# One copy, a reordered entry and an earlier split: three edits at the transitions of a fused recurrence, attention and projection kernel

## The chip, the cores and the metric

The kernel runs on one core of a Trainium2 chip. The metric is the device time of one execution in microseconds (us), as the median of several runs. Names of engines: PE is TensorE (PEld its weight loads), DVE is VectorE, ACT is ScalarE, POOL is GpSimd, SP is SyncE, which here issues nearly all DMA transfers. Each engine works through its own instructions in order; semaphores make one wait for another.

## The reference

One layer on x of 2048 tokens by 1024 (a grid of 32 rows by 64 columns), float32:

```python
mod = silu(c) @ ada_w + ada_b                    # shift, scale, gate
h = layernorm(x) * (1 + scale) + shift
proj = h @ w_in                                  # 1024 -> 9216 columns
q_h, i_h, zf_fw, zf_bw, g_h, q_n, k_n, v_n, g_n = split(proj)

# HGRN2, 8 heads of 128, forward and backward in time, in chunks of 32 tokens
f = lb + (1 - lb) * sigmoid(zf);  k = 1 - f
state = decay * state + k_end^T v                # per chunk
o = q_inter @ state + tril(q k^T) v              # decays folded into q and k
y_hg = rmsnorm(o_fw + o_bw) * silu(g_h)

# neighbourhood attention, 16 heads of 64, windows of 8 x 16 inside the grid
s = q k^T / 8 + bias (masked);  p = softmax(s)
y_na = (p @ v) * silu(g_n)

y = concat(y_hg, y_na) @ w_out                   # 2048 -> 1024
out = layernorm(alpha * x + gate * y) * ln_g + ln_b
```

## The kernel before

Float32 products are made from a high and a low half of each operand: three matmuls (high x high, high x low, low x high) of 128 x 128 by 512 or 256 columns. ScalarE makes the high half by a copy (`wh`, `yh`, `wo`, L268, L1460, L1428), VectorE the low half by a subtraction (`wl`, `yl`, L269, L1461, L1429).

The program has five stages: layernorm, modulation and the first half of attention (to about 530 us); 16 HGRN units, 8 heads times two halves of the sequence (530 to 1740); the second half of attention, 8 units of two heads (1740 to 2296); and the output projection, whose first four row tiles run inside the last attention unit.

**Who sets the order.** PE's instructions run in the order in which the program writes them (`manual_schedule`). A function `weave` advances two generators in turn: a mixer (one HGRN or attention unit) and a stream of dense matmuls (projections of the next unit), so that the dense ones fill PE while the mixer waits for other engines. The instructions of ACT, DVE and SP are ordered by a scheduler with priorities; `tc.high_priority(offset=PRI)` puts one ahead, and `pinned` (which is `keep_in_program_order`) keeps it in the order of the program with the other pinned ones of its engine.

**The first HGRN unit.** `hgrn` works in two groups g of four chunks of 128 tokens. `turned` (L472, L474) transposes the decayed keys into `ke`. `updates` (L480) multiplies ke and v for four chunks into one PSUM tile "pu", of which there is one buffer. `forward_states` (L485 to L494) then makes four states on DVE: the first one by a copy (L493), the others by decay times the state before plus the chunk's part of "pu" (L491). A second `updates` for the other direction needs the same buffer, and so comes after the fourth state step. In between stand `diagonal_factors` (kx and qx, L504 to L510) and after it `diagonal` (L519); then come `level` (L547), `masked` (pm, L560) and `outputs` (L571, L573).

**The second half of attention.** A unit `Prep` has q, k and gate prepared from projection results (`q`: L950 and L951, `k`: L966 and L967, `gate`: L984 to L986), and loads its value tiles (`v`: L977). `alone` (L758) makes Z, a copy of one head's queries. `vproj` projects the values (L291): eight steps of 24 matmuls at a pair of heads' columns, each four steps ending with two evacuations `vt` (L297). `vstream` gives these steps one by one; before attention starts, five of them run, in the middle of which two evacuations come. Then `natten_woven` walks through 16 places (R, j) per unit: `scores` (L1029 to L1036 on PE, bias and maximum on DVE L1045, exponential on ACT L1050, normalising on DVE L1055), two places later `turned` (transposes of the probabilities, L1078, copied to pt on DVE L1082 and ACT L1084) and `sums` (L1100). Tables of places call further work in between (`extra`):

```python
extra = {..., 7: [(wo_split, 0, 0, 1)], 8: [(wo_split, 0, 2, 3), (wo_load, 0, 6, 7)],
         9: [(wo_split, 0, 4, 5)], 10: [(wo_load, 1, 0, 1, 4, 5), (y_early, 0)], 11: [(y_early, 1)]}
```

**The start of the output projection.** `y_early` (L1434) loads the gated results y of one row tile as two pieces from DRAM, `y_split` (L1460, L1461) halves them, `wo_load` and `wo_split` (L1428, L1429) do the same for w_out. The matmuls of y (L1468 to L1470) are the dense stream of attention's last unit, u = 7. Both of the first tiles are split at the start of that unit.

Of the kernel before, what the change touches and what calls it, by code (L numbers as in the profile page):

```python
# [13 lines left out]
AF = mybir.ActivationFunctionType  # L14
# [16 lines left out]
PRI = 1500  # L31
# [7 lines left out]
def body(ctx: ExitStack, tc: tile.TileContext, t):  # L39
    nc = tc.nc  # L40
    dve, act, pool, pe = nc.vector, nc.scalar, nc.gpsimd, nc.tensor
    dma = nc.sync.dma_start
    x, out = t["x"], t["out"]
# [236 lines left out]
    def vproj(src, dst, half, feed=None, fine=False):  # L280
        his, los = feed.take(4) if feed else load_split(lambda i: src[:, i * 512:(i + 1) * 512], 4)
        for t2 in range(2):
            pzs = [ps("pj"), ps("pj")]
            for k in range(KT):
                wh, wl = (w[k // 2][:, (k % 2) * 256:(k % 2 + 1) * 256] for w in (his, los))
                for tp in range(2):
                    for i in range(2):
                        g, o = divmod(((t2 * 2 + tp) * 2 + i) * P, GRP)
                        hh, hl = (hts[g, k, s][:, o:o + P] for s in range(2))
                        for n, (a, b) in enumerate(((hh, wh), (hh, wl), (hl, wh))):  # L290
                            pe.matmul(pzs[tp][:, i * 256:(i + 1) * 256], a, b, start=(k == 0 and n == 0 and i == 0), stop=(k == KT - 1 and n == 2), skip_group_check=True)  # L291
                if k % 2:
                    if k == KT - 1:
                        for tp, pz in enumerate(pzs):
                            v = tl("vo")
                            with tc.high_priority(offset=PRI):
                                act.activation(v, pz, AF.Copy)  # L297
                                r0 = half * HALF + (t2 * 2 + tp) * 256
                                dma(dst[r0:r0 + 256].rearrange("(i p) c -> p i c", p=P), v.rearrange("p (i c) -> p i c", c=256))
                    if feed and t2:  # L300
                        feed.free(1)
                if fine or k % 2:
                    yield None
# [117 lines left out]
    def hgrn(u, half, st, tail):  # L421
# [55 lines left out]
        def updates(ke, v):  # L477
            pu = ps("pu")
            for b in range(4):
                pe.matmul(pu[:, b * P:(b + 1) * P], ke[:, b * P:(b + 1) * P], v[:, b * P:(b + 1) * P], start=True, stop=True)  # L480
            return pu
# [94 lines left out]
        for g in range(2):  # L576
            v = turned(vts[g], "v")
            next(tail, None)
            cs, ks = {}, {}
            cs[0], ks[0] = rates(0, g)  # L580
            yield 5
            next(tail, None)
            cs[1], ks[1] = rates(1, g)
            de0 = ends(0, g, cs[0], ks[0])
            yield 5
            next(tail, None)
            ke0 = turned(de0, "ke")
            de1 = ends(1, g, cs[1], ks[1])
            kx, qx = diagonal_factors(g, cs, ks)
            yield 3  # L590
            next(tail, None)
            forward_states(g, updates(ke0, v))
            ke1 = turned(de1, "ke")
            yield 3
            next(tail, None)
            pu = updates(ke1, v)
            if g == 0:
                ub = tl("ub")
                act.activation(ub, pu, AF.Copy)
                ubs[g] = ub  # L600
            else:
                ubs[g] = pu
            pb = diagonal(kx, qx)
            lf = [(w, *level_factors(w, g, cs, ks)) for w in (32, 64)]
            yield 6
            next(tail, None)
            pa = ps("pa")
            for w, xk, xq in lf:
                level(w, pa, xk, xq)
            pm = masked(pa, pb)  # L610
            yield 5
            outputs(g, v, pm)
# [139 lines left out]
    def alone(st, R):  # L752

        z = keysets[0]["Z"]
        with tc.high_priority(offset=PRI):
            for hh in range(2):
                hs_ = slice(hh * 64, hh * 64 + 64)
                act.activation(z[hs_, hh * 512:(hh + 1) * 512], st.Q[R][hh][hs_], AF.Copy)  # L758

    NCOL = (("q", 5120), ("k", 6144), ("g", 8192))  # L760
    NCOL0 = (("k", 6144), ("q", 5120), ("g", 8192))
# [140 lines left out]
    NLEN = 2 * len(NCOL) * KT * KUS  # L902
    VLEN = 8 * 2.9
# [22 lines left out]
    class Prep:  # L926


        def __init__(self, p, half, raws):
            self.p, self.half, self.raws = p, half, raws  # L930
            self.Q, self.V, self.sg, self.bias, self.bk = {}, {}, {}, {}, {}

        def fetch(self, name):
# [10 lines left out]
        def q(self, R):  # L944
            raw = self.src("q", R)
            rv = raw.rearrange("p (r j c) -> p j r c", j=4, c=16)[:, :, ::-1, :]
            a, b = tl("Q", F32R), tl("Q", F32R)
            av, bv = (z.rearrange("p (j r c) -> p j r c", j=4, c=16) for z in (a, b))
            keep = pinned if raw is self.bk.get("q") else lambda x: x
            keep(act.activation(av[0:64], rv[0:64], AF.Copy))  # L950
            keep(act.activation(bv[64:128], rv[64:128], AF.Copy))  # L951
            dve.tensor_tensor(av[64:128], rv[0:64], av[0:64], op=ALU.subtract)
            dve.tensor_tensor(bv[0:64], rv[64:128], bv[64:128], op=ALU.subtract)
            self.Q[R] = (a, b)

        def k(self, i):
            a, b, src, off = KPIECE[self.half][i]
            n = (b - a) * GW
            raw = (self.bk[src] if src in self.bk else self.raws["k"][src])[:, off:off + n]
            o = slice(a * GW, b * GW)  # L960
            top, bot = slice(0, 64), slice(64, 128)
            keys = keysets[self.p % len(keysets)]
            keep = pinned if src in self.bk else lambda x: x
            for z, x, y in (("KA", top, bot), ("KB", bot, top)):
                z = keys[z]
                keep(act.activation(z[x, o], raw[x], AF.Copy))  # L966
                dma(z[y, o].bitcast(F32), z[x, o].bitcast(F32))  # L967
                dve.tensor_tensor(keys["KL"][x, o], raw[x], z[x, o], op=ALU.subtract)
# [11 lines left out]
        def gate(self, R):  # L980
            raw = self.src("g", R)
            sg = tl("sg")
            keep = pinned if raw is self.bk.get("g") else lambda x: x
            keep(act.activation(sg, raw, AF.Exp, scale=-1.0))  # L984
            sigmoid(sg)
            dve.tensor_tensor(sg, raw, sg, op=ALU.mult)  # L986
            self.sg[R] = sg
# [545 lines left out]
    with psum_phase("n1", NPS), phase("n1", NB1, SM1), tc.manual_schedule(engines={mybir.EngineType.PE}):  # L1533
        natten_init(4, 1)
        st = st0
        for f, *a in ((st.k, 0), (st.k, 1), (st.k, 2), (st.q, 1), (alone, st, 1), (st.table, "mid", 0), (st.table, "mid", 1), (st.v, 2), (st.v, 3), (st.table, "mid", 3), (st.q, 2), (st.v, 4), (st.gate, 1)):
            f(*a)
        vs = vstream(2, 3)
        for _ in range(5):
            next(vs)  # L1540
        pipe = []
        cts = [(c + u * P) // P for u in range(1, 8) for _ in range(2 if u == 7 else 1) for n, c in NCOL]
        feed = Feed(cts)
        feed.at = 0
        for u in range(8):
            nxt, extra = None, None
            if u < 7:
                raws, dense = natten_stream(u + 1, 1, feed, u + 1 == 7)
                total = NLEN
                if u == 0:  # L1550
                    dense, total = chain(vs, dense), NLEN + 1.375 * VLEN
                nxt = Prep(u + 1, 1, raws)
                if u == 6:
                    extra = {4: [(wo_load, 0, 0, 1)], 5: [(wo_load, 0, 2, 3, 4, 5)], 7: [(wo_split, 0, 0, 1)], 8: [(wo_split, 0, 2, 3), (wo_load, 0, 6, 7)],
                             9: [(wo_split, 0, 4, 5)], 10: [(wo_load, 1, 0, 1, 4, 5), (y_early, 0)], 11: [(y_early, 1)]}
            else:
                y_split(0, 1)
                dense, total = out_stream(list(range(NE))), NE * 16 * KUS
                extra = {0: [(wo_split, 0, 6, 7), (wo_load, 1, 2, 3)], 1: [(wo_split, 1, 0, 1), (wo_load, 1, 6, 7)], 2: [(wo_split, 1, 2, 3, 4, 5)], 3: [(wo_split, 1, 6, 7)]}
            weave(natten_woven(st, nxt, pipe, extra), dense, total, 24)  # L1560
            st = nxt
        m, r, c, pts = pipe.pop(0)
        m.sums(r, c, pts)
        turn(pipe, 1)
        m, r, c, pts = pipe.pop(0)
        m.sums(r, c, pts)
# [72 lines left out]
```

## Time and profile before

| | us |
|---|---|
| runs, median of 3 (lowest to highest) | 2625.78 (2624.72 to 2625.88) |
| profiled execution | 2628.06 |
| its span | 2626.3 |
| PE busy | 2562.5 (98%) |
| PE weight loads busy | 2149.1 (82%) |
| DVE busy | 1738.8 (66%) |
| ACT busy | 1434.5 (55%) |
| POOL busy | 108.7 (4%) |
| mean granted clock of PE | 0.992 |

Rows of the timeline give start (us), duration (us), engine, line, operation, out<-in, shapes, count, and in brackets the engine's idle time before it with what ended it. "x8" on a row means eight such instructions in a row and their time together. Rows of stretches give the stretch, its length, the busy time of PE, PEld, DVE, ACT and POOL with the number of instructions, then the granted clock (1.00 is full speed), the DMA share and GB/s. Rows of waits give who waited for whom: us in total, times, the longest.

### The profile page before, as it was taken

Reading aid. Unit: us, or ns where it says so; the run is one execution under the profiler, and the core shown is the slowest. Engines: PE = TensorE matmul, PEld = TensorE weight load, DVE = VectorE, ACT = ScalarE, POOL = GpSimd, SP = SyncE. Lnnn points to the kernel's source line nnn. Section 1 sums busy time; section 2 is a strip of 40 time slices with the busy share of each in tenths; the row PEclk is TensorE's granted clock in tenths of the full one; section 3 lists DMA queues with packets and bytes.
Section 4 is the critical chain, followed back from the end, with each engine's and each line's share of the span. In section 5 each row is a group of like instructions: output and inputs, shape, how many; then the busy total and the mean of one; then the engine's idle time right before and its main releaser. Section 6 shows DMA issues by size and latency. Waiting matters only on the chain.

```text
span 2626.3 us, 45803 instructions
## 1 busy us (share of the span) xinstructions
PE 2562.5 (98%) x17140; PEld 2149.1 (82%) x17140; DVE 1738.8 (66%) x4354; ACT 1434.5 (55%) x2856; POOL 108.7 (4%) x143
## 2 busy tenths in 40 slices
PE   6999999989999999999999999999999998999998
PEld 5888888878888888888888888888888886788887
DVE  7444545477777778877887787555777778558443
ACT  4534444366666566666766666454677777431110
POOL 0000000000000000000000000000000000042221
PEclk9999999999999999999999999999999999999999
DMA  7476454212111126212122222344455546443331
GB/s 272 141 212 143 133 169 154 93 48 71 65 64 58 65 69 219 84 52 78 65 64 67 74 75 75 109 144 129 122 143 139 147 133 172 125 153 129 97 97 57
DMA packets 225631, 295.87 MB, mean 113 GB/s; under 512 B 28807, under 2 KB 117511, under 8 KB 224263
## 3 DMA queue, kind: packets, MB, share of 16 engines
q1 hardware_dynamic: 225407, 292.93, 36.5%
q8 instruction: 135, 2.21, 0.4%
q14 instruction: 89, 0.73, 0.1%
HBM read 217.65 MB, written 66.99 MB: 108 GB/s over the span
## 4 chain that ended last, share of the span: by engine, by line
PE 72%; DVE 2%; DMA 2%; ACT 2%; issue 0%; DVEq 0%; SPq 0%; ACTq 0%
PE pj L278 39%; PE ps L1468 4%; PE ps L1469 4%; PE ps L1470 4%; PE pj L291 2%; PE ps L1100 2%; PE ps L1078 2%; PE ps L480 2%; PE ps L472 2%; PE ps L547 1%; PE ps L1029 1%; PE ps L571 1%; PE ps L573 1%; PE ps L519 1%; PE ps L645 1%; DMA bias<-tint 1%
## 5 line engine op out<-in xcount | busy, mean ns | idle before, releaser
L278 PE MATMUL pj<-h,wh 128*128 128x512 f32 x4000 | 1273.6, 399 | 4.2 <-ACT wh L817 1.9
L278 PEld LDWEIGHTS pj<-h,wh 128*128 128x128 f32 x4000 | 725.4, 188 | 156.4 <-issue 13.8
L278 PE MATMUL pj<-h,wl 128*128 128x512 f32 x2000 | 783.9, 392 | 0.0
L278 PEld LDWEIGHTS pj<-h,wl 128*128 128x128 f32 x2000 | 375.6, 188 | 83.4 <-DVE wl L793 0.4
L1050 ACT ACTIVATE pbuf<-pbuf,mx 128x480 f32<-128x480 f32 (+5 forms) x256 | 152.5, 597 | 116.5 <-DVE mx L1045 115.5
L291 PE MATMUL pj<-wh,h 128*128 128x256 f32 x1024 | 198.4, 288 | 4.1 <-ACT vt L297 3.8
L1045 DVE CUSTOM_DVE_ANT_1 pbuf<-ps,bias 128x480 f32<-128x480 f32 (+5 forms) x256 | 129.1, 540 | 110.0 <-PE ps L1036 46.7
L291 PEld LDWEIGHTS pj<-wh,h 128*128 128x128 f32 x1024 | 165.2, 194 | 7.9 <-ACT vt L297 4.5
L268 ACT ACTIVATE wh<-wr 128x512 fp32r<-128x512 f32 x192 | 120.3, 626 | 79.2 <-PE pj L278 68.9
L269 DVE TENSOR_TENSOR wl<-wr,wh 128x512 fp32r<-128x512 f32 x192 | 131.3, 684 | 48.1 <-ACT wh L268 47.9
L291 PE MATMUL pj<-wl,h 128*128 128x256 f32 x512 | 145.9, 285 | 0.0
L1084 ACT ACTIVATE pt<-ps 120x384 f32<-120x384 f32 (+3 forms) x128 | 65.2, 509 | 118.9 <-PE ps L1078 118.5
L1082 DVE COPY pt<-ps 120x384 f32<-120x384 f32 (+3 forms) x128 | 74.9, 585 | 66.0 <-PE ps L1078 65.0
L1078 PE MATMUL ps<-ident,pbuf 128*128 128x128 f32 (+2 forms) x832 | 113.7, 274 | 4.5 <-DVE pbuf L1055 3.4
L1078 PEld LDWEIGHTS ps<-ident,pbuf 128*128 128x128 f32 (+2 forms) x832 | 97.3, 137 | 22.8 <-ACT pbuf L1050 3.8
L466 DVE TENSOR_TENSOR de<-e,de 128x512 f32<-128x512 f32 x64 | 44.2, 691 | 94.4 <-ACT de L465 94.4
L1444 ACT ACTIVATE yh<-yr 128x512 fp32r<-128x512 f32 x52 | 32.7, 628 | 132.6 <-PE ps L1469 115.4
L766 ACT ACTIVATE e<-pj 128x512 f32<-128x512 f32 x98 | 58.3, 595 | 85.2 <-PE pj L278 78.0
L1055 DVE TENSOR_SCALAR pbuf<-pbuf,mx 128x480 f32<-128x480 f32 (+5 forms) x256 | 101.0, 412 | 3.9
L1517 DVE TENSOR_TENSOR vt<-ps,gt 128x512 f32<-128x512 f32 x24 | 16.5, 691 | 129.2 <-PE ps L1470 129.2
L291 PEld LDWEIGHTS pj<-wl,h 128*128 128x128 f32 x512 | 99.3, 194 | 1.4 <-issue 0.5
L447 DVE TENSOR_TENSOR_SCAN c<-c,g 128x128 f32<-128x128 f32 x256 | 88.4, 404 | 10.7 <-ACT c L437 10.7
(274 smaller groups left out, 4681.6 us busy)
## 6 DMA issues: line engine op xcount, KB each, us to landing
wr<-in_w_in SPq DMA_DIRECT2D x276, 256.0 KB
yr<-yq SPq DMA_DIRECT2D x64, 256.0 KB
bias<-tint SPq DMA_DIRECT2D x24, 480.0 KB
x<-in_x SPq DMA_DIRECT2D x32, 256.0 KB
ada<-in_ada_m SPq DMA_DIRECT2D x8, 1024.0 KB
wr<-in_w_v SPq DMA_DIRECT2D x32, 256.0 KB
nv<-vt SPq DMA_DIRECT2D x32, 256.0 KB
hs<-s SPq DMA_DIRECT2D x32, 256.0 KB
```

The source lines that it names most:

```text
L268: act.activation(hi, raw, AF.Copy)
L269: dve.tensor_tensor(lo, raw, hi, op=ALU.subtract)
L278: pe.matmul(pz, a, b, start=(k == 0 and n == 0), stop=(k == KT - 1 and n == 2))
L291: pe.matmul(pzs[tp][:, i * 256:(i + 1) * 256], a, b, start=(k == 0 and n == 0 and i == 0), stop=(k == KT - 1 and n == 2), skip_group_check ...
L447: dve.tensor_tensor_scan(c[:, sl], c[:, sl], L[:, sl], 0.0, op0=ALU.add, op1=ALU.subtract)
L1045: return dve.tensor_tensor_reduce(s[:, 0:nk].rearrange("p (r c) -> p r c", c=kw), sc[:, 0:nk].rearrange("p (r c) -> p r c", c=kw), bt[:, 0 ...
L1050: act.activation(s[:, 0:nk], s[:, 0:nk], AF.Exp, scale=-1.0, bias=mx[:, 0:1], accum_out=mx[:, 1:2])
L1055: dve.tensor_scalar(s[:, 0:nk], s[:, 0:nk], mx[:, 2:3], 1.0, op0=ALU.mult, op1=ALU.mult)
L1078: pe.transpose(ptp[0:cw, c * P:(c + 1) * P], s[:, c * cw:(c + 1) * cw], ident)
L1468: pe.matmul(pz, yh[:, kk], wh, start=first, stop=False)
L1469: pe.matmul(pz, yh[:, kk], wl, start=False, stop=False)
L1470: pe.matmul(pz, yl[:, kk], wh, start=False, stop=last)
```

## The change

Three places are changed.

First, in unit 0 of the first half, group 0, the PSUM tile of the forward updates is copied by ACT at high priority into a tile `held` (tag "t"), and the four state steps read the copy.

Second, at the entry of attention's second half: the ACT copies of q, k and gate of the half's first unit (`self.first`), Z of that unit and the value evacuations of that half are pinned to the order of the program; q and gate of R = 2 and 1 move behind four value steps; six value steps instead of five run ahead of attention, and the dense length given to `weave` falls from 1.375 to 1.25 times VLEN.

Third, the loads of the first two row tiles of y are called one place earlier in unit 6, and the split of tile 0 is called at place 10 of unit 6 instead of at the start of unit 7.

```diff
                         for tp, pz in enumerate(pzs):
                             v = tl("vo")
                             with tc.high_priority(offset=PRI):
-                                act.activation(v, pz, AF.Copy)
+                                (pinned if half else lambda x: x)(act.activation(v, pz, AF.Copy))
...
             next(tail, None)
-            forward_states(g, updates(ke0, v))
+            pu = updates(ke0, v)
+            if u + half + g == 0:
+                held = tl("t")
+                with tc.high_priority(offset=PRI):
+                    act.activation(held, pu, AF.Copy)
+                pu = held
+            forward_states(g, pu)
             ke1 = turned(de1, "ke")
...
-                act.activation(z[hs_, hh * 512:(hh + 1) * 512], st.Q[R][hh][hs_], AF.Copy)
+                (pinned if st.first else lambda x: x)(act.activation(z[hs_, hh * 512:(hh + 1) * 512], st.Q[R][hh][hs_], AF.Copy))
...
             self.p, self.half, self.raws = p, half, raws
+            self.first = half and p == 0
...
-            keep = pinned if raw is self.bk.get("q") else lambda x: x
+            keep = pinned if raw is self.bk.get("q") or self.first else lambda x: x
...
-            keep = pinned if src in self.bk else lambda x: x
+            keep = pinned if src in self.bk or self.first else lambda x: x
...
-            keep = pinned if raw is self.bk.get("g") else lambda x: x
+            keep = pinned if raw is self.bk.get("g") or self.first else lambda x: x
...
-        for f, *a in ((st.k, 0), (st.k, 1), (st.k, 2), (st.q, 1), (alone, st, 1), (st.table, "mid", 0), (st.table, "mid", 1), (st.v, 2), (st.v, 3), (st.table, "mid", 3), (st.q, 2), (st.v, 4), (st.gate, 1)):
+        for f, *a in ((st.k, 0), (st.k, 1), (st.k, 2), (st.q, 1), (alone, st, 1), (st.table, "mid", 0), (st.table, "mid", 1), (st.v, 2), (st.v, 3), (st.table, "mid", 3), (st.v, 4)):
             f(*a)
         vs = vstream(2, 3)
-        for _ in range(5):
+        for _ in range(4):
+            next(vs)
+        st.q(2)
+        st.gate(1)
+        for _ in range(2):
             next(vs)
...
-                    dense, total = chain(vs, dense), NLEN + 1.375 * VLEN
+                    dense, total = chain(vs, dense), NLEN + 1.25 * VLEN
...
-                             9: [(wo_split, 0, 4, 5)], 10: [(wo_load, 1, 0, 1, 4, 5), (y_early, 0)], 11: [(y_early, 1)]}
+                             9: [(y_early, 0), (wo_split, 0, 4, 5)], 10: [(y_split, 0), (wo_load, 1, 0, 1, 4, 5), (y_early, 1)]}
             else:
-                y_split(0, 1)
+                y_split(1)
```

The order of ACT in the first HGRN unit, before; c, ei, g, e and de are the decays and gates of the next groups, ke the transposed keys:

```order
L453 ACTIVATE ei_5745<-c_5701 128x512
L474 ACTIVATE ke_5509<-ps_5504 128x512
L439 ACTIVATE g_5738<-g_5734,l1m 128x512
L435 ACTIVATE g_6072<-e_5384 128x512
L377 ACTIVATE e_5523<-pj_5478 128x512
```

And after (lines behind the edit are 6 or 7 higher):

```order
L453 ACTIVATE ei_5747<-c_5703 128x512
L596 ACTIVATE t_5496<-ps_5491 128x512
L474 ACTIVATE ke_5511<-ps_5506 128x512
L439 ACTIVATE g_5740<-g_5736,l1m 128x512
L435 ACTIVATE g_6074<-e_5384 128x512
L377 ACTIVATE e_5525<-pj_5478 128x512
```

The copy (L596, out of PSUM into t) stands between ei and ke; the rows around it are the same.

The order of ACT at the entry of attention's second half, before, from the pair of Q of R = 1 to the two evacuations of values (vt):

```order
L950 ACTIVATE Q_18682<-bk_17364 64x512
L951 ACTIVATE Q_18683<-bk_17364 64x512
L950 ACTIVATE Q_18706<-e_17934 64x512
L951 ACTIVATE Q_18707<-e_17934 64x512
L984 ACTIVATE sg_18717<-bk_17370 128x512
...
L984 ACTIVATE sg_19353<-e_18304 128x512
L758 ACTIVATE Z_18661<-Q_18682 64x512
L758 ACTIVATE Z_18661<-Q_18683 64x512
L297 ACTIVATE vt_18845<-pj_18747 128x512
L297 ACTIVATE vt_18848<-pj_18748 128x512
```

And after:

```order
L957 ACTIVATE Q_18684<-bk_17366 64x512
L958 ACTIVATE Q_18685<-bk_17366 64x512
L764 ACTIVATE Z_18663<-Q_18684 64x512
L764 ACTIVATE Z_18663<-Q_18685 64x512
L297 ACTIVATE vt_18835<-pj_18737 128x512
L297 ACTIVATE vt_18838<-pj_18738 128x512
L957 ACTIVATE Q_18841<-e_17936 64x512
L958 ACTIVATE Q_18842<-e_17936 64x512
L991 ACTIVATE sg_18847<-bk_17372 128x512
```

Z and vt follow the first pair of Q at once; the second pair of Q and the gate come after them.

The order of DVE at the end of unit 6, before, from the low halves of keys (KL) to the 288 columns of probabilities (pbuf) and the sigmoid steps (sg, L337):

```order
L1054 RECIPROCAL mx_24658<-mx_24658 128x1
L1054 RECIPROCAL mx_24663<-mx_24663 128x1
L1045 ISA pbuf_18650,mx_24738<-ps_24732,bias_24501 128x360
L1045 ISA mx_24738 128x1
L1045 ISA pbuf_18652,mx_24743<-ps_24733,bias_24501 128x360
L1045 ISA mx_24743 128x1
L1055 TENSOR_SCALAR pbuf_18654<-pbuf_18654,mx_24658 128x288
L1055 TENSOR_SCALAR pbuf_18656<-pbuf_18656,mx_24663 128x288
L337 TENSOR_SCALAR sg_24706<-sg_24706 128x512
```

And after, with the two yl of tile 0 about the maximum step of these 288 columns:

```order
L1468 TENSOR_TENSOR yl_24647<-yr_24580,yh_24646 128x512
L1052 ISA pbuf_18656,mx_24672<-ps_24666,bias_24425 128x288
...
L1468 TENSOR_TENSOR yl_24651<-yr_24582,yh_24650 128x512
...
L1061 RECIPROCAL mx_24677<-mx_24677 128x1
L337 TENSOR_SCALAR sg_24720<-sg_24720 128x512
L1062 TENSOR_SCALAR pbuf_18656<-pbuf_18656,mx_24672 128x288
```

Before, all four yl stood behind these rows. On ACT the two yh of tile 0 stand before the keys of unit 7 (KA, KB); before, they stood behind the sigmoid steps. The order of PE changes at one place: 24 matmuls of the value projection (one step) now stand ahead of the first scores of the half and no longer behind a later place. On SP the loads of V, bias and bk of the half's first unit stand behind two stores of vt and between weight loads wr, which stood behind them before.

## The prediction

> **What bounds the kernel now.** I read the busy times first, then TensorE's waits, then three places in the timeline, each with the rows by stretch for the granted clock.
>
> ```profile
> PE 2562.5 (98%) x17140; PEld 2149.1 (82%) x17140; DVE 1738.8 (66%) x4354; ACT 1434.5 (55%) x2856; POOL 108.7 (4%) x143
> ```
>
> TensorE works for 98% of the span, about 64 us of it are empty, and no other engine passes 66%. An edit that leaves TensorE's instructions alone can gain only where TensorE stands still, or runs slowly because it stood still. The list of its waits (us in total, times, longest) has these among its largest rows:
>
> ```profile
> PE ps L480 <- DVE Sf L491: 8.1, 1, 8.1
> PE pj L1468 <- ACT yh L1460: 7.4, 2, 6.2
> ...
> PE pj L291 <- ACT vt L297: 3.8, 1, 3.8
> ```
>
> The 8.1 us wait is the first HGRN unit's second chain of state updates, the 3.8 us the value projection at the entry of attention's second half, the 6.2 us the first row tile of the output projection. The three edits sit at these places; I call them A, B and C. The total number of matmuls doesn't change, so the forecast is a sum over three places.
>
> **A, states from a copy.** The stretches around the stop, cut at steps of 3.413 us (us, then busy us of PE, PEld, DVE, ACT and POOL, then PEclk):
>
> ```profile
> 554.35:557.76 3.41, 1.29 (x6) 0.74 (x4) 3.41 (x9) 3.41 (x8) 0.00 (x0) 1.00 0.03 11
> 557.76:561.17 3.41, 0.00 (x0) 0.00 (x0) 3.41 (x11) 2.90 (x8) 0.00 (x0) 0.50 0.20 66
> ...
> 564.58:568.00 3.42, 3.42 (x72) 3.04 (x72) 0.86 (x3) 1.44 (x3) 0.00 (x0) 0.50 0.02 5
> 568.00:571.41 3.41, 3.41 (x16) 2.82 (x16) 2.64 (x6) 2.41 (x3) 0.00 (x0) 1.00 0.00 0
> ```
>
> A stretch in which TensorE was busy for 1.29 of 3.41 us is followed by one at clock 0.50, and the full rate returns at 568.00, after a full stretch at half rate. So a stop costs its own length and the slow matmuls behind it:
>
> ```profile
> 563.77 2.05 PE L480 MATMUL ps<-v,ke 128*128 128x128 f32 x8 [8.14 <-DVE Sf L491]
> 565.75 1.51 PE L519 MATMUL ps<-qx,kx 128*32 128x64 f32 x64
> 567.19 1.08 PE L278 MATMUL pj<-h,wh 128*128 128x512 f32 x2
> ...
> 600.06 1.06 PE L480 MATMUL ps<-v,ke 128*128 128x128 f32 x8
> 601.05 0.91 PE L519 MATMUL ps<-qx,kx 128*32 128x64 f32 x64
> ```
>
> TensorE stops at 563.77 - 8.14 = 555.63. The same eight updates take 1.06 us at 600.06 and the 64 diagonal products 0.91, so half rate costs 0.99 + 0.60, and about 0.4 on the next pair: 2.0 us.
>
> ```profile
> 556.68 0.59 ACT L474 ACTIVATE ke<-ps 128x512 f32<-128x512 f32 x1
> ...
> 556.30 0.28 DVE L493 COPY Sf<-ps 128x128 f32<-128x128 f32 x1
> ...
> 559.55 1.29 DVE L510 TENSOR_TENSOR kx<-kx,e 128x512 f32<-128x512 f32 x2
> ```
>
> The added copy has the size and the kind of ScalarE's ke (PSUM to SBUF, 128x512, 0.59 us), and stands directly ahead of it. It runs at 556.68 to 557.26 and frees the one PSUM buffer; ke ends near 557.75 instead of 557.27, and the second updates start near 557.85. The stop shrinks from 8.1 to 2.2 us. What is late next is kx: the diagonal products need L510, which ended at 560.84. VectorE is without a gap there (3.41 of 3.41 us), and one state copy (0.28) and a part of a state step now come behind it, so I take 560.4. TensorE then waits 0.7 to 1.6 us more. The dense matmuls, before at 567.19 and worth 567.6 at full rate, start at 561.65 if the clock is back at 561.17, a gain of 5.9; if half rate holds to the next boundary at 564.58 they start at 562.0 and lose 1.3 more: 4.3.
>
> ```profile
> 567.39 0.30 DVE L557 COPY_PREDICATED pdb<-mskd,ps 128x128 f32<-128x128 uint32 x1 [2.56 <-issue]
> ...
> 577.37 1.17 DVE L560 TENSOR_TENSOR pm<-pdb 32x128 f32<-32x128 f32 x4
> ...
> 580.54 0.61 PE L571 MATMUL ps<-pm,v 128*128 128x128 f32 x4
> ```
>
> A cap comes from VectorE, which is the busier engine here. TensorE's sums at 580.54 need pm, which VectorE ended at 578.54. VectorE can move forward only by its idle time before it: 2.56 us at 567.39 and some 0.7 more, 3.2 us. So pm comes at 575.3 at the earliest, and TensorE can't be more than 5.2 us early there. **A: 4.8 us, from 4.0 to 5.2.** The lower end has kx 0.3 later than the cold case. ScalarE's extra 0.59 us is covered: it was busy for 1.44 of the 3.42 us from 564.58.
>
> **B, entry of attention's second half.**
>
> ```profile
> 1747.82 1.15 ACT L984 ACTIVATE sg<-e 128x512 f32<-128x512 f32 x2
> 1748.87 1.26 ACT L758 ACTIVATE Z<-Q 64x512 fp32r<-64x512 f32 x2
> 1750.16 1.08 ACT L297 ACTIVATE vt<-pj 128x512 f32<-128x512 f32 x2
> ...
> 1746.73 0.28 PE L291 MATMUL pj<-wh,h 128*128 128x256 f32 x1
> 1750.81 0.58 PE L291 MATMUL pj<-wh,h 128*128 128x256 f32 x1 [3.80 <-ACT vt L297]
> ```
>
> TensorE ended its fifth value step at 1747.01 and needs the PSUM buffers that vt empties. ScalarE did two gates and two Z behind a row of Q, KA and KB first, and came to vt at 1750.16. The changed order puts Z and vt directly behind the first pair of Q, and moves the groups between them behind. So vt waits for TensorE alone: one vt is 0.54 us, and with the hand-over I expect TensorE back at 1747.75, a wait of 0.75. That is 3.05 us. The cold part, from the value matmuls by themselves (us, PE, PEld, PEclk):
>
> ```profile
> 1744.00:1747.00 3.00, 3.00 (x26) 2.81 (x24) 1.00 0.70 145
> 1750.80:1756.00 5.20, 5.19 (x24) 5.13 (x24) 0.52 0.32 93
> ```
>
> A step of 24 took 5.19 us at half rate; at full rate 24 x 3.00 / 26 = 2.8. A stop of 0.75 us leaves any stretch of 3.41 us busy for 2.7, more than the 1.29 that was followed by half rate, so these 2.3 us go as well. The sixth value step is the same work moved ahead of the first scores, and costs nothing by itself; it also gives the keys, the bias and the displaced Q and gate a step's time (2.8 us). **B: 5.35 us, from 4.3 to 5.6**; the lower end has a second wait of 1 us behind the displaced Q or gate.
>
> **C, start of the output projection.**
>
> ```profile
> 2225.88 0.49 PE L1034 MATMUL ps<-KL,Z 128*128 128x360 f32 x2
> 2232.53 0.79 PE L1468 MATMUL pj<-wo,yh 128*128 128x512 f32 x1 [6.17 <-ACT yh L1460]
> ...
> 2236.54 1.10 PE L1078 MATMUL ps<-ident,pbuf 128*96 128x128 f32 x6
> ...
> 2241.22 0.39 PE L1100 MATMUL ps<-pt,V 96*64 96x128 f32 x4
> ...
> 2249.17 1.04 PE L1078 MATMUL ps<-ident,pbuf 128*128 128x128 f32 x8
> ...
> 2231.86 1.14 ACT L1460 ACTIVATE yh<-yr 128x512 fp32r<-128x512 f32 x2
> ...
> 2235.12 0.63 ACT L1460 ACTIVATE yh<-yr 128x512 fp32r<-128x512 f32 x1 [0.57 <-DMA yr<-yq]
> ...
> 2237.74 0.47 ACT L1084 ACTIVATE pt<-ps 96x384 f32<-96x384 f32 x1
> ...
> 2228.69 0.64 DVE L1055 TENSOR_SCALAR pbuf<-pbuf,mx 128x288 f32<-128x288 f32 x2
> ...
> 2232.60 1.28 DVE L1461 TENSOR_TENSOR yl<-yr,yh 128x512 fp32r<-128x512 f32 x2
> ```
>
> TensorE stops at 2226.36 and has nine matmuls of y next, then six transposes of probabilities. Tile 0's split now runs a unit earlier, so those nine go at once and end near 2228.4 (9 x 3.41 / 16, from A's last stretch, is 1.9). Much of the 6.2 us comes back as three waits. First, VectorE's normalising of 288 columns ended at 2229.33; the two yl (1.28) and a sigmoid step now stand ahead of it, so it ends at 2230.3 and 2231.3: TensorE waits 1.95 + 0.65. Second, the scores move from 2239.56 to 2233.85, but the next sums need pt from ScalarE, still behind tile 1's yh, whose load lands at 2235.12: pt at about 2237.2 instead of 2238.2, a wait of 1.7. Third, VectorE's low half of w_out block 6, behind tile 1's yl, comes near 2238.9: 0.8. From there the old order runs on, with the transposes of 2249.17 at 2245.7. **C: 3.4 us**; 5.1 if only the first wait is real, 1.5 if tile 1's load or the clock takes two more. [...]
>
> [...]
>
> **Sum.** 4.8 + 5.35 + 3.4 = 13.55 us. The profiled execution took 2628.06 with a span of 2626.3 and stands 2.3 us above the median of 2625.78; the same difference from the median gives **2612.3 us** (profiled 2614.5, span 2612.8). About 0.2%, 5.25 us, is what a measurement tells from no change.
>
> **Rivals.**
>
> C is given back. VectorE and ScalarE are both full around 2230; if the three waits eat the gain, C is 0 and the time is 2625.78 - 10.15 = 2615.6. For it: the two engines that make the waits had no slack in the stretch of the stop:
>
> ```profile
> 2226.88:2230.29 3.41, 0.00 (x0) 0.00 (x0) 3.35 (x14) 3.41 (x9) 0.00 (x0) 1.00 1.02 225
> ```
>
> Against: 6 us of stop can't return without one of them being half again as long as its rows say. 0.14.
>
> A or B is lost on VectorE. If pm or the displaced Q and gate on VectorE (B) holds TensorE by as much as the copy frees, one term goes: about 2617.5. For it: VectorE has 3.2 us to give in A. Against: in B it isn't the engine waited for. 0.10.
>
> [...]
>
> Slower: values late in B. SyncE issues in order, and the changed order puts two stores of vt and weight loads, which wait for a buffer, ahead of loads of the value tiles V.
>
> ```profile
> 1747.67 8.96 SPq L977 DMA_DIRECT2D V<-nv  x8
> ...
> 1778.63 0.39 PE L1100 MATMUL ps<-pt,V 120*64 120x128 f32 x4
> ...
> 2224.69 1.25 SPq L1434 DMA_DIRECT2D yr<-yq  x2
> ```
>
> The first eight V were issued by 1756.63, and the first sums that read V run at 1778.63, or 1773.3 once TensorE is 5.35 early. A load of y issued at 2224.69 was waited for until 2235.12, so I allow 10 us to land. V issued after 1763 delays TensorE one for one; at 1777 it takes the 13.5 us back (no gain), and at 1782 it is slower by over 0.2%. At 1790 the time is 2638. Against it: that is 33 us behind the old issue, and a weight buffer comes free with each split, every few us. 0.04.
>
> The change doesn't do it: the scheduler leaves the copy, vt and yh late. 2625.8. ScalarE's rows show all three early, so only a late input (tile 0's load) could. 0.06.
>
> **How the numbers follow.** Forecast 0.62; C given back 0.14; one of A and B lost 0.10; the other clock rule 0.04; no effect 0.06; slower 0.04. Faster is 0.62 + 0.14 + 0.10 + 0.04 = 0.90, same 0.06, slower 0.04. The terms' own ends give 9.8 to 15.9 us, 2609.9 to 2616.0; the range reaches down to 2608, for waits of B or C that turn out shorter together with the other clock rule, and up to 2618.5 to take in the two partial losses.
>
> **What would show it.** After the change TensorE's list of waits should have no row of 8 us at L480, but about 2.2 us there and about 1 at L519; under 1 us at L291 for vt; no 6 us row for yh, but about 2.6 us for pbuf of the 288 columns, 1 to 2 for pt of 96 rows, and under 1 for w_out's low half. The stretch at 1748 to 1756 should show clock 1.00. The busy time of TensorE should fall by 4 to 5 us (matmuls no longer at half rate) and its idle time by some 8 to 10. A wait of over 3 us that isn't in the old list, above all for V, or at the sums near 575, would make the forecast wrong, as would a stop at L480 that still ends with L491.

## The result and the profile after

The whole change ran at a median of 2617.34 us (2614.5 to 2619.83, 6 runs) against 2625.83 (2624.72 to 2628.62, 6 runs): a ratio of 0.9966, 95% interval 0.9953 to 0.9978, or 8.5 us. Later, on another occasion, it ran at 2616.15 (5 runs) against 2625.58 (15 runs), ratio 0.9965 (0.9953 to 0.9978). It is faster, inside the range on record (2608 to 2618.5), with 5 us less than the 13.5 that were forecast. Both medians lie above 2616.0, where the forecast's own terms end: it is the margin for partial losses that takes them in. The profiled execution took 2618.81 us with a span of 2617.0:

```profile
PE 2561.1 (98%) x17140; PEld 2146.7 (82%) x17140; DVE 1736.9 (66%) x4354; ACT 1435.0 (55%) x2857; POOL 108.5 (4%) x143
```

TensorE's waits after the change (us in total, times, longest):

```profile
PE ps L1107 <- ACT pt L1091: 5.5, 1, 5.5
PE ps L1085 <- DVE pbuf L1062: 3.3, 2, 1.7
PE ps L480 <- ACT ke L474: 3.0, 2, 2.2
...
PE ps L1036 <- DMA V<-nv: 1.7, 1, 1.7
PE ps L519 <- DVE kx L510: 1.5, 1, 1.5
PE pj L1475 <- ACT yh L1467: 1.2, 1, 1.2
```

The rows of 8.1 us for Sf, 3.8 for vt and 6.2 for yh are gone. In A there are the two small waits that were forecast (2.2 for ke, 1.5 for kx). Two rows are larger than forecast or new: 5.5 us for pt, where 1.7 was forecast, and 1.7 at the first scores of attention's second half, where none was. The forecast had said that a wait of over 3 us that isn't in the old list would make it wrong; the one for pt is such a wait.

To see where the time went, I took the start of the same matmul in both traces and subtracted: a negative number is TensorE's lead over the trace of before (us). Each column is the change of that lead across one place, so that a piece of bad luck elsewhere stays out of it. "w_out" is a place near 2200 that the forecast didn't name (below). The column of B ends near 2100 and that of C at 2400, so that late effects are in; small rests lie between the places.

| trace | up to A | A | B | w_out | C | end |
|---|---|---|---|---|---|---|
| the whole change | +1.6 | -4.7 | -4.7 | -3.2 | +2.0 | -9.2 |
| the whole change, again | +3.3 | -4.4 | -4.7 | -3.0 | -1.8 | -11.0 |
| A only | -0.5 | -4.4 | +0.6 | -3.2 | +1.8 | -6.3 |
| B only | -0.1 | 0.0 | -6.2 | -3.4 | -0.1 | -10.6 |
| C only | 0.0 | +0.2 | -1.3 | -3.0 | +0.5 | -3.6 |
| A and B | +2.3 | -4.7 | -4.4 | -3.4 | +3.7 | -8.0 |
| change, split behind pt | +1.4 | -4.7 | -3.6 | -3.4 | -3.6 | -14.7 |
| change, y load ahead of w_out | +0.2 | -4.4 | -2.3 | -3.4 | +2.5 | -8.2 |
| both of these | +2.3 | -5.2 | -4.1 | -2.6 | -0.7 | -9.0 |
| change, second table late | +1.1 | -4.7 | +3.8 | -3.4 | -0.2 | -3.8 |
| split behind pt, table behind keys | +0.4 | -4.4 | -6.6 | -3.4 | -4.6 | -17.3 |
| C only, split behind pt | +1.6 | -0.3 | -0.6 | -3.4 | -4.1 | -7.7 |

The rows without an edit show how far one trace can be trusted at its place. Traces without A move by up to 0.3 us in column A, those without B by -1.3 to +0.6 in column B, and those without C by -0.1 to +3.7 in column C. So column A can be read as it stands, and a single entry of column C can't.

**A in the trace after.**

```profile
559.44 1.16 PE L480 MATMUL ps<-v,ke 128*128 128x128 f32 x8 [2.19 <-ACT ke L474]
562.07 1.39 PE L519 MATMUL ps<-qx,kx 128*32 128x64 f32 x64 [1.47 <-DVE kx L510]
...
577.45 0.61 PE L571 MATMUL ps<-pm,v 128*128 128x128 f32 x4
```

```profile
558.84:562.25 3.41, 1.33 (x22) 1.15 (x26) 3.41 (x11) 3.41 (x10) 0.00 (x0) 1.00 0.21 77
562.25:565.66 3.41, 3.41 (x69) 2.90 (x62) 3.41 (x10) 1.92 (x4) 0.00 (x0) 0.50 0.02 5
```

The sums of this unit start at 577.45, and before at 580.54: 3.1 us earlier, though TensorE came to this place 1.6 us later than in the trace of before. VectorE is without a gap in both stretches, as the working had it. Half rate does come, for one stretch instead of three, after a stretch in which TensorE was busy for 1.33 us.

**B in the trace after.**

```profile
1742.82 1.32 ACT L297 ACTIVATE vt<-pj 128x512 f32<-128x512 f32 x2 [2.50 <-PE pj L291]
1744.16 0.63 ACT L957 ACTIVATE Q<-e 64x512 fp32r<-64x512 f32 x1
...
1751.19 0.40 PE L1036 MATMUL ps<-KA,Q 128*128 128x360 f32 x1 [1.71 <-DMA V<-nv]
```

ScalarE now waits for TensorE at vt, and TensorE doesn't wait for vt at all. The first scores wait 1.71 us for a DMA. The profile's inference names V, but these matmuls read KA, whose other half is copied by a DMA:

```profile
1738.32 1.30 SPq L730 DMA_DIRECT2D bias<-tint  x2
1739.71 0.52 SPq L974 DMA_DIRECT2D KA<-KA  x1
```

Two bias tables go first, 480 KB each, then the copies of keys.

**C in the trace after.**

```profile
2214.69 0.49 PE L1041 MATMUL ps<-KL,Z 128*128 128x360 f32 x2
2215.02 0.39 PE L1475 MATMUL pj<-wo,yh 128*128 128x512 f32 x1
...
2219.00 0.51 PE L1085 MATMUL ps<-ident,pbuf 128*96 128x128 f32 x3 [1.73 <-DVE pbuf L1062]
2219.95 0.51 PE L1085 MATMUL ps<-ident,pbuf 128*96 128x128 f32 x3 [0.44 <-DVE mx L1061]
...
2229.92 0.47 PE L1107 MATMUL ps<-pt,V 96*64 96x128 f32 x1 [5.51 <-ACT pt L1091]
```

```profile
2215.83 1.25 SPq L1441 DMA_DIRECT2D yr<-yq  x2
```

```profile
2226.10 0.63 ACT L1467 ACTIVATE yh<-yr 128x512 fp32r<-128x512 f32 x1 [4.82 <-DMA yr<-yq]
2227.82 0.63 ACT L1467 ACTIVATE yh<-yr 128x512 fp32r<-128x512 f32 x1 [1.10 <-DMA yr<-yq]
...
2229.40 0.47 ACT L1091 ACTIVATE pt<-ps 96x384 f32<-96x384 f32 x1
```

The first matmuls of y follow at once, the 6.2 us stop is gone, and the waits for pbuf (1.73 and 0.44) are near the 1.95 and 0.65 of the working. Then ScalarE stands for 4.82 and 1.10 us at tile 1's split, whose load has not landed, with the copy of pt behind it, and TensorE stands for 5.51 us at the sums. In the stretch of that stop VectorE and ScalarE were busy for 0.69 and 0.77 of 3.41 us:

```profile
2224.55:2227.96 3.41, 0.00 (x0) 0.00 (x0) 0.69 (x1) 0.77 (x2) 0.00 (x0) 1.00 0.83 192
```

**The place near 2200.** Here the trace of before is the odd one. The list of waits before has a row there that the prediction didn't use:

```profile
PE ps L1078 <- DVE pbuf L1055: 3.4, 1, 3.4
```

```profile
2200.98 0.63 ACT L1428 ACTIVATE wo<-vt 128x512 fp32r<-128x512 f32 x1 [3.17 <-DMA vt<-in_w_out]
```

ScalarE waited 3.17 us for a load of w_out, and TensorE 3.4 for what stood behind it, with a stretch of half rate after it (2206.39 to 2209.80, clock 0.50). All twelve other profiles, B only and C only among them, have this wait at 1.3 to 2.1 us and gain about 3 us there; in eleven of them (all but B only) the six transposes behind the wait take 0.84 us, and before they took 1.50. So the profiled execution of before was 3 us unlucky at one place. That hardly enters the comparison of medians, but it does enter a comparison of two single traces.

### The profile page after: what moved, and what is told of

Its sections match the earlier page's. It is cut to its first block, busy times and chain, and to the rows that moved or that the text cites. A ratio compares the mean times of both kernels' runs of the same rounds, so it can differ in the third digit from the quotient of the medians.

```text
span 2617.0 us, 45804 instructions
## 1 busy us (share of the span) xinstructions
PE 2561.1 (98%) x17140; PEld 2146.7 (82%) x17140; DVE 1736.9 (66%) x4354; ACT 1435.0 (55%) x2857; POOL 108.5 (4%) x143
## 4 chain that ended last, share of the span: by engine, by line
PE 90%; DVE 4%; DMA 3%; ACT 2%; issue 1%; SPq 0%; DVEq 0%; ACTq 0%
PE pj L278 51%; PE pj L291 5%; PE ps L1475 4%; PE ps L1477 4%; PE ps L1476 4%; PE ps L1107 3%; PE ps L1085 3%; PE ps L480 2%; PE ps L472 2%; PE ps L1036 1%; PE ps L547 1%; DMA bias<-tint 1%; PE ps L571 1%; PE ps L1043 1%; PE ps L573 1%; PE ps L519 1%
```

## The experiments

The theory after the first comparison (theory 1 below): A gives what was forecast; B gives about 1.7 us less, which go to a new wait for keys; C's gain goes back, because ScalarE works in order and pt stands behind tile 1's split. Each "only" kernel has the other parts of the diff undone.

**A only.** The kernel before with this edit alone:

```diff
-            forward_states(g, updates(ke0, v))
+            pu = updates(ke0, v)
+            if u + half + g == 0:
+                held = tl("t")
...
+            forward_states(g, pu)
```

> Only part A (states from a copy). Theory 1 (read off the trace after the change: A gave 4.9 us there, from +1.6 to -3.3 of TensorE's lead): 2625.8 - 4.9 = 2621, a wait of about 2.2 us at the second updates and 1.5 us at the diagonal products, no wait for Sf. Theory 2 (A only shifts VectorE's work and is given back at pm near 575): within 1 us of before.

2621.31 us (11 runs) against 2626.34 (27 runs), ratio 0.9982 (0.9974 to 0.9991): 5.0 us, and 4.4 at the place itself. The waits are 2.2 for ke and 0.6 for kx, and TensorE's wait for pm is 0.6. Theory 1 holds; nothing is given back at pm.

**B only.** The kernel before with the pins, the new list of calls, the sixth value step and the new length:

```diff
+            self.first = half and p == 0
...
-        for _ in range(5):
+        for _ in range(4):
+            next(vs)
+        st.q(2)
+        st.gate(1)
+        for _ in range(2):
```

> Only part B (ScalarE's order and six value steps). Theory 1: the vt wait and its half rate go (6.2 us), but the first scores then wait 1.7 us for keys that are copied by DMA, so 2625.8 - 4.4 = 2621.4. Theory 2 (as forecast, the wait for keys is an accident of the one trace): 2620.4 and no wait at the first scores.

2620.57 us (11 runs) against the same 2626.34, ratio 0.9983 (0.9974 to 0.9991): 5.8 us, with a wait of 0.18 at the first scores:

```profile
1752.87 0.41 PE L1030 MATMUL ps<-KA,Q 128*128 128x360 f32 x1 [0.18 <-DMA V<-nv]
```

The theory of the forecast was right for B alone. A wait of more than 0.2 us for keys appears only with A: it is 1.9 us with A and B. With A, TensorE reaches the first scores 3.2 us earlier (1749.48 against 1752.69), but the keys' copies are issued only 1.5 us earlier (1739.71 against 1741.18 in this trace):

```profile
1741.18 0.52 SPq L968 DMA_DIRECT2D KA<-KA  x1
```

**C only.** The kernel before with these:

```diff
-9: [(wo_split, 0, 4, 5)], 10: [(wo_load, 1, 0, 1, 4, 5), (y_early, 0)], 11: [(y_early, 1)]}
+9: [(y_early, 0), (wo_split, 0, 4, 5)], 10: [(y_split, 0), (wo_load, 1, 0, 1, 4, 5), (y_early, 1)]}
-                y_split(0, 1)
+                y_split(1)
```

> Only part C (tile 0 of y split a unit earlier). Theory 1: what the early tile gives (about 8 us) goes back, because ScalarE stands at tile 1's split, whose load has not landed, with the copy of pt behind it: a wait of 3 to 5.5 us at the sums, and a total within 2 us of before, 2624 to 2627.5. Theory 2 (as forecast): the wait for pt is under 2 us and the time is 2622.4.

2625.05 us (11 runs) against 2626.34, ratio 0.9997 (0.9988 to 1.0006): no difference that can be told. The wait for pt is there, 2.9 us.

```profile
PE ps L1100 <- ACT pt L1084: 2.9, 1, 2.9
```

**A and B, without C.** The changed kernel with the diff of C only taken back.

> Parts A and B without C. Theory 1 (C is worth nothing or costs up to 2 us): 2615 to 2617, not above the whole change's 2617.3. Theory 2 (C gains its 3.4 us and A or B gives less): 2619.5 to 2621, above the whole change by 2 to 3.4 us.

2616.09 us (5 runs) against 2626.34, ratio 0.9961 (0.9948 to 0.9975): 10.3 us. This is not above the whole change (2617.34 and 2616.15). C adds nothing that these runs can tell to A and B, though the 6.2 us wait for yh is whole again here. The alternative on record, 2619.5 to 2621, is out. The late load of tile 1 costs TensorE something even without C once A and B have moved it forward: VectorE's low half of tile 1 stands ahead of its part of pt, and TensorE waits 2.0 us for that.

```profile
PE pj L1475 <- ACT yh L1467: 7.4, 2, 6.2
...
PE ps L1107 <- DVE pt L1089: 2.3, 2, 2.0
```

The profiled execution is the slowest of the five here (2620.47), so its +3.7 in column C is rather high.

**Tile 1's split behind pt.** The edit, against the changed kernel:

```diff
-                y_split(1)
                 dense, total = out_stream(list(range(NE))), NE * 16 * KUS
-                extra = {0: [(wo_split, 0, 6, 7), ...
+                extra = {"t0": [(y_split, 1)], 0: [(wo_split, 0, 6, 7), ...
...                                  # in natten_woven, behind turn(pipe, 2):
+            for f, *a in extra.get("t%d" % i, []):
+                f(*a)
```

Each yh is pinned. By ScalarE's order in the traces this places it behind the instruction written just before it on its engine, and not, as said above, in one order with all the other pinned ones. Written right behind the turn, it comes after pt.

> The whole change, but tile 1 of y is split after the copy of pt on ScalarE instead of before it. Theory 1 (C's gain went back because pt stood behind tile 1's split, which waits for its load): the 5.5 us wait at the sums and the half rate behind it go, 2617.3 - 6 = 2611.3, range 2609.5 to 2613. Theory 2 (the load itself is what TensorE waits for): the wait moves to tile 1's first matmuls, and the time stays within 2 us of the whole change, 2615.5 to 2618.

2613.43 us (5 runs) against 2625.97 (15 runs), ratio 0.9954 (0.9941 to 0.9968): 12.5 us. ScalarE's rows, to be read against those of the change:

```profile
2222.36 0.48 ACT L1091 ACTIVATE pt<-ps 96x384 f32<-96x384 f32 x1
2224.77 0.63 ACT L1469 ACTIVATE yh<-yr 128x512 fp32r<-128x512 f32 x1 [1.94 <-DMA yr<-yq]
2226.20 0.63 ACT L1469 ACTIVATE yh<-yr 128x512 fp32r<-128x512 f32 x1 [0.80 <-DMA yr<-yq]
```

The load still lands late (issued at 2214.44, split at 2224.77 and 2226.20), but nothing that TensorE needs soon stands behind it, and the wait for pt isn't in the list any more. TensorE gains 3.6 us across the place in this trace; in the first trace of the change it lost 2.0, in the second it gained 1.8. The interval overlaps that of the change, so the medians alone (12.5 us against 8.5 and 9.4) don't separate the two kernels; the rows do, since the wait is gone and didn't move to tile 1's first matmuls. Theory 1 holds, some 2 us short of its middle.

**Tile 1's loads ahead of w_out's.**

```diff
-10: [(y_split, 0), (wo_load, 1, 0, 1, 4, 5), (y_early, 1)]
+10: [(y_split, 0), (y_early, 1), (wo_load, 1, 0, 1, 4, 5)]
```

> The whole change, but tile 1's two loads of y are called ahead of the four loads of w_out at the same place. Theory 1: ScalarE's order is the same, so the wait at the sums shrinks by what the load lands earlier, 2 to 4 us of 5.5; 2613.5 to 2615.5. Theory 2 (landing is set by traffic, not by the place in the queue): no change, 2617.

2617.35 us (5 runs) against 2625.97, ratio 0.9967 (0.9954 to 0.9979): no better than the change. Theory 2 has the time, but neither theory has the reason. The wait for pt went entirely, and TensorE's lead was 15.2 us at 2244, but only 8.2 at 2400:

```profile
2249.52 0.79 PE L1475 MATMUL pj<-wo,yh 128*128 128x512 f32 x1 [3.23 <-ACT wo L1435]
```

```profile
2248.84 0.63 ACT L1435 ACTIVATE wo<-vt 128x512 fp32r<-128x512 f32 x1 [4.06 <-DMA vt<-in_w_out]
```

Loads of w_out are late instead, and ScalarE stands at them; behind the wait TensorE's next six matmuls of 512 columns take 0.63 to 0.80 us, where those ahead of it took 0.39 to 0.50. The late loads aren't the four that the edit moved back, which were split by 2239. The load waited for at 2248.84 was issued only at 2245.82, and in the run above, where TensorE's lead was about the same (15.5 us), at 2241.74:

```profile
2245.82 0.33 SPq L1430 DMA_DIRECT2D vt<-in_w_out  x1
```

```profile
2241.74 0.33 SPq L1432 DMA_DIRECT2D vt<-in_w_out  x1
```

Why it goes out later, these runs don't show.

**Both edits.** The two diffs above together.

> Both edits of the two runs beside it: tile 1's split behind pt, and its loads ahead of w_out's. Theory 1: with the wait for pt gone there is little left for the earlier load, 2610 to 2612. Theory 2: it is the earlier load alone that helps, as in the run beside it, 2613.5 to 2615.5.

2617.12 us (5 runs; 2612.3 to 2618.85) against 2625.97, ratio 0.9963 (0.9951 to 0.9976). Neither theory named this. The lead of 13.1 us at 2260 falls to 9.0 behind a wait for w_out, after which six matmuls of 512 columns take 0.63 to 0.80 us (0.39 or 0.40 ahead of it):

```profile
PE pj L1477 <- ACT wo L1437: 2.1, 1, 2.1
```

The earlier load gains nothing with either order of ScalarE. That it does harm is not shown: with the split behind pt the medians differ by 3.7 us, but the intervals overlap.

**Second bias table later.** The call moves behind four value steps:

```diff
-(alone, st, 1), (st.table, "mid", 0), (st.table, "mid", 1), (st.v, 2), ...
+(alone, st, 1), (st.table, "mid", 0), (st.v, 2), ...
...
+        st.table("mid", 1)
         st.q(2)
```

> The whole change, but the second bias table of attention's second half is called after four value steps, so that its 480 KB do not stand ahead of the copies of keys. Theory 1 (B lost 1.7 us at the first scores because the copied keys landed behind two bias tables): the wait at the first scores goes, 2615.6. Theory 2 (the copies are late for another reason, or the table comes late for the second scores): 2617 or more.

2624.29 us (11 runs) against 2625.97, ratio 0.9993 (0.9985 to 1.0002): nearly all of the change's gain is lost. The wait at the first scores is gone, and there is one of 7.6 us later:

```profile
PE ps L1036 <- DVE mx L1052: 7.6, 1, 7.6
```

```profile
1757.05 3.47 SPq L730 DMA_DIRECT2D bias<-tint  x1
```

The table's load went out only at 1757, behind stores and value tiles, and VectorE could not add it to the second scores. Both theories have a part: the keys were late because of what stands ahead of them, and this is no place for the table. The keys were issued here at the same time as in the change (1739.73 against 1739.71), behind one table and a small load of V instead of two tables, and the first scores start without a wait:

```profile
1739.73 0.52 SPq L974 DMA_DIRECT2D KA<-KA  x1
```

```profile
1749.49 0.33 PE L1036 MATMUL ps<-KA,Q 128*128 128x360 f32 x1
```

The last copy of KA was issued at 1742.25 here and at 1742.28 in the change. There it landed at 1750.94, by the semaphore times in the trace, and the first scores started at 1751.19 behind a wait of 1.71; here they start at 1749.49 without one. So the second table alone, 480 KB ahead of the keys, is enough for that wait.

**Split behind pt, and the second table behind the keys.** Beside the split behind pt, the first table is called ahead of the keys, and the second one's load is pinned behind the instruction written before it on SyncE:

```diff
-for f, *a in ((st.k, 0), (st.k, 1), (st.k, 2), (st.q, 1), (alone, st, 1), (st.table, "mid", 0), (st.table, "mid", 1), ...
+for f, *a in ((st.table, "mid", 0), (st.k, 0), (st.k, 1), (st.k, 2), (st.q, 1), (alone, st, 1), (st.table, "mid", 1), ...
...
-            dma(bf, table_ap(tint[p], 22, jt, 8, 0, 15))
+            (pinned if behind else lambda x: x)(dma(bf, table_ap(tint[p], 22, jt, 8, 0, 15)))
```

> The whole change with tile 1's split behind pt (the faster kernel of the last runs), and the second bias table queued behind the copies of keys and two stores of values, ahead of the value tiles. Theory 1 (keys are late only because two tables of 480 KB stand ahead of them): the 1.7 to 2.6 us wait at the first scores goes and the table still lands before the second scores, 2613.4 - 1.7 = 2611.7. Theory 2 (the table is late there too): a wait at the second scores instead, 2613.4 or more.

2611.54 us (5 runs; 2610.0 to 2615.15) against 2625.58 (15 runs), ratio 0.995 (0.9936 to 0.9963): 14 us, the fastest median here. It is 4.6 us below the whole change that was run beside it (2616.15); from the 12.5 us of the split behind pt alone the runs don't tell it apart.

```profile
1735.77 0.64 SPq L730 DMA_DIRECT2D bias<-tint  x1
1736.46 0.55 SPq L984 DMA_DIRECT2D V<-nv  x1
1737.11 0.52 SPq L974 DMA_DIRECT2D KA<-KA  x1
...
1744.47 0.66 SPq L730 DMA_DIRECT2D bias<-tint  x1
```

The keys go 2.6 us earlier than in the change, though TensorE's lead ahead of B differs by only 0.8 us; the first scores start at 1748.49 without a wait, and TensorE gains 6.6 us across B. Its list of waits has no row for V, and none for ScalarE's pt. Two things help the keys here: one table less ahead of them, and an earlier issue, since SyncE, which in the change stood for 1.7 us ahead of its two tables, doesn't stand there. The run before this one shows that the first is enough to end the wait.

**C only, with the split behind pt.** The diffs of C only and of the split behind pt, on the kernel before.

> Only part C, with tile 1's split behind the copy of pt; A and B undone. Theory 1 (C was worth nothing only because pt stood behind tile 1's split): about 4 us faster than before, 2621 to 2622.5. Theory 2 (the gain of that order needs the lead that A and B give): within 1.5 us of before.

2622.35 us (11 runs) against 2625.58, ratio 0.9986 (0.9977 to 0.9994): 3.2 us, where C alone without that order gained nothing that can be told. The intervals of these two overlap a little; the lists of waits don't: 2.9 us for pt in C only, and no such row here. So the order of ScalarE decides about that wait, with or without the lead of A and B.

**The whole change once more.**

> The whole change once more, on the chip of the two runs beside it, to set them against: 2617.3, range 2615.5 to 2618.5, with a wait of 3 to 5.5 us for pt at the start of the output projection.

2616.15 us, with a shorter wait for pt than expected:

```profile
PE ps L1107 <- ACT pt L1091: 2.2, 1, 2.2
```

In this trace TensorE gains 1.8 us across C; in the first it lost 2.0. The size of the wait is set by when two loads land, and differs between these two executions of one kernel by 3.3 us.

## Why the prediction was right, and where it was not

**What bounds it: right.** The gains came where TensorE had stood. In the trace its busy time fell by 1.4 us (2562.5 to 2561.1), less than the 4 to 5 forecast, because other stretches at half rate came: at 279 us (below) and at 2228, behind the wait for pt (clock 0.50 from 2227.96 to 2234.78).

**A: right, with its working.** 4.8 us forecast; 4.4 to 5.2 at the place in the nine traces that have A, 5.0 between the medians of A alone. The wait of 2.2 for ke was exact; kx was 0.6 to 1.5 late, where 0.7 to 1.6 was forecast. The trace of both edits gained 5.2, the forecast's upper end.

**B: the stop right, what is late next missed.** 5.35 was forecast, and B alone is worth 5.8. The working named the keys, the bias and the displaced Q and gate as having a step's time; it did not set the keys' landing against a TensorE that A had already moved 3 us forward. That costs 1.7 us in both traces of the change, and the lower bound (a second wait of 1 us) was for another engine. The slower rival looked at the same queue, but at V: V's loads did go later (the first of them at 1750.0 instead of 1747.7), and TensorE's list of waits has no row of sums for them.

**C: the step that failed is the wait for pt.** 1.7 us was forecast and 5.5 and 2.2 were measured. The working kept tile 1's landing where it was relative to the sums. In the trace TensorE came to this place 11.2 us earlier than before (2214.69 against 2225.88), the load's issue only 8.9 us earlier (2215.83 against 2224.69), and the two loads were waited for until 10.3 and 12.0 us after it instead of 9.2 and 10.4. 2.3 and 1.6 more on 1.7 make 5.6. The mechanism (a wait for pt behind tile 1's yh) and the wait before it were as written; the third wait, for w_out's low half, was not there. Part of the miss is there without A and B: C only has 2.9 us for pt. In sum C gave nothing that can be told instead of 3.4. The rival "C is given back" had the price (2615.6), through that one of its three waits, but not the reason: it argued that VectorE and ScalarE are full there, and ScalarE stood idle for 4.82 us at a load. The working's own terms also add up a little differently from what it wrote: 5.7 us for the scores less 1.7 and 0.8 is 3.2, not 3.4, and 5.7, not 5.1, with the first wait alone (in B, 5.19 less 2.8 is 2.4, not 2.3).

**The sum.** By medians A alone gives 5.0, B alone 5.8 and C alone 1.3: together 12.1, each with an interval of about 2.3 us either way. The whole change gave 8.5 and 9.4. A and B together gave 10.3 of their 10.8, so by medians little is lost between them, and the rest of the difference lies within the intervals. The traces show two losses that the forecast lacked, B's keys behind A (1.7 us) and C's longer wait for pt; what each takes from the median is not shown. The forecast's centre was 4 to 5 us too low. That the range held owes something to luck: its margin for partial losses was argued from a full VectorE and ScalarE, and the losses that came were late loads.

**The clock.** The forecast gives 0.04, and part of the lower end of its range, to another clock rule; no run shows that term. What the runs showed in its place is a stretch at half rate in A behind one with 1.33 us of work, where before it followed 1.29.

## What to carry to other kernels

An engine that works in order hands on a late load to everything queued behind it, as ScalarE's 4.82 us at tile 1's load came out as 5.51 us of TensorE at the sums: a split of an operand that isn't needed yet belongs behind the copies that are needed now. When several edits each move the bounding engine forward, ask at each later place what did not move with it, above all the queue of transfers. A load put ahead can make those behind it late though they are issued no later, as the second table did to the keys (a wait of 1.7 us). An earlier load of y gained nothing in these runs.

## What the hardware showed that I had not expected

Most of the stretches ahead of half rate held some work of TensorE. Between 100 and 2600 us the traces of before and of the change have seven places where the granted clock falls to 0.50. TensorE was busy in the 3.41 us ahead of them for 1.29, 1.42, 0.65 and 0.00 us before (the stretches from 554.35, 1745.59, 2202.98 and 2226.88) and for 1.52, 1.33 and 0.00 us after (from 275.53, 558.84 and 2224.55). At half rate the same matmuls take about twice as long (the eight updates of A took 2.05 us instead of 1.06).

One of the seven is a difference between equal pieces of work. At 279 us, far from any edit, the trace of the change has a stretch at half rate, and that of before has none:

```profile
278.95:282.36 3.41, 3.41 (x9) 2.67 (x9) 1.22 (x3) 0.34 (x1) 0.00 (x0) 0.50 0.74 226
```

It costs 1.5 us: TensorE's lead goes from +0.2 to +1.7. The stop ahead of it has the same length in both traces, 1.90 us, and ends at 278.11 before and at 278.29 after:

```profile
278.29 0.73 PE L278 MATMUL pj<-h,wh 128*128 128x512 f32 x2 [1.90 <-ACT wh L823]
```

After, all of it lies between 275.53 and 278.95, where TensorE was busy for 1.52 us, and the clock behind is 0.50. Before, its last 0.26 us lie behind 277.85; from 274.44 to 277.85 TensorE was busy for 1.77 us and from there to 281.27 for 3.16, and the clock stays at 1.00. So here the same stop of less than two microseconds cost 1.5 us more in one trace than in the other. A median over runs evens this out; a pair of traces doesn't.
